# Attention stage: stores at the end of a step, a load queue in written order, norm weights at a group's turn

## The chip, the cores and the metric

The kernel runs on one core of a Trainium2 chip. A core has a matrix engine (TensorE, PE in the profile, with its weight loads as PEld), a vector engine (DVE), a scalar engine (ACT), a general engine (POOL) and a synchronisation engine (SP), which here does nothing but give out DMA transfers. Each engine takes its instructions strictly in the order in which they stand in its queue; semaphores tie the queues together. The metric is the device time of one execution in microseconds (us).

## The reference

One decoder layer on x of 2048 x 1024 in float32. The input is normalised and multiplied by one wide matrix. One branch is a chunked gated DeltaNet (after a short causal convolution); the other is a dilated sliding-window attention in three groups of four heads, which are merged by their softmax denominators. Both are gated, projected, merged by sigmoid gates, projected once more and added to x. What matters here is the attention branch:

```python
h = rms_norm(x, norm_w[layer])
proj = h @ w_in[layer]
...
sq = partial_rope(rms_norm(grp(swa_q), q_norm_w[layer][:, None, :]), cos, sin)
sk = partial_rope(rms_norm(grp(swa_k), k_norm_w[layer][:, None, :]), cos, sin)
sv = grp(swa_v)
for gi, (window, dilation) in enumerate(SWA_GROUPS):
    o_g, lse_g = dilated_window_attention(sq[:, :, gi], sk[:, :, gi], sv[:, :, gi], window, dilation)
```

The norm weights of queries and keys (q_norm_w, k_norm_w) differ by group, not by head. The dilations are 1, 4 and 16, so a block of 128 queries of groups 1 and 2 takes rows that lie 4 or 16 apart; the kernel therefore writes the projected rows to memory and reads them back in the order that the attention wants.

## The kernel before

Products of float32 are made of three products in a faster format: each operand is split into a high part (hh, wh) and a low part (hl, wl), and high x high, high x low and low x high are summed (L238 to L240). The high part is a copy on ACT, the low part a subtraction on DVE or POOL.

The attention stage is made of 12 units, a unit being one head of one group, with the groups in the order 2, 1, 0. A unit has 16 steps t, one per block of 128 rows, and a step has four parts j. Each part projects two of the eight k tiles (`s_proj`: 384 columns, queries, keys and values at once). In a step's part 1 the block of the step before gets its turn (`s_turn`: DVE multiplies by the inverse norm and the norm weights wqk, POOL applies the rotation in four instructions) and is stored (rscr<-rec). At the end of a step `s_norm` reads the projection: ACT takes the squares and the copy into rec, of which there are two buffers, and POOL makes the inverse norm. So the squares of step k + 2 wait until the store of step k has landed.

Attention blocks run between the parts of a step, some steps behind (`att_add` gives each its step, `at`): with d the step less `at`, the rows are loaded at d = -2 (qk<-rscr, v<-rscr), transposed at d = 0, scored at d = 1; at d = 2 the probabilities are transposed and multiplied with v, DVE copies the result into ol, and it is stored (oscr<-ol). What is left when the 12 units are done runs between the products of the next stage.

In the first unit the step also prepares x, one tile x(c) of 128 rows after the other (a list xq of events with their due quarter step). `x_next` takes ACT's squares of xt and POOL's power; `x_diag` puts the inverse norms on a diagonal (dg, ACT); `x_event` is a small PE product that spreads them over all partitions (tp, L120), followed by eight scalings on DVE (xc, L126); `x_parts` makes hh on ACT (L131) and hl in two pieces on DVE and POOL (L135), and then gives out the load of x(c + 3), whose buffer is free once hl of x(c) is made. `swa_first` does this for x(0) and splits the first unit's eight weight tiles (`high` on ACT, `low` on DVE for even and on POOL for odd tiles, L193).

The next unit's weights come in six raw tiles of 256 KB (`w384`, a generator that a step advances: in the first unit from step 12 on, in the others from step 6). There are three raw buffers.

PE, ACT, DVE and POOL follow the order in which the program is written (a manual schedule, switched on by `pinned`). In `swa_first` so does SP; in `swa_units` SP is left to the scheduler, which may give out a transfer earlier or later than it is written, as its dependencies allow.

## Time and profile before

| | |
|---|---|
| median of 3 runs | 2385.1 us (2384.5 to 2389.4) |
| the profiled execution | 2384.28 us, span 2382.4 us |
| PE busy, share of the span | 2343.1 us, 98% |
| ACT, DVE, POOL busy | 36%, 50%, 37% |
| share of the chain that ended last | PE 85%, POOL 4%, DMA 4%, DVE 4%, ACT 2% |
| mean granted TensorE clock | 0.996 |
| DMA | 307.30 MB, 129 GB/s over the span |

The attention stage covers about the first 1,020 us of the span. PE's busy time contains the overlap of matmuls that follow each other, so a busy PE is one that has no hole, not one at its peak. A row of a timeline has the start and the length in us, the engine, the line of the kernel, what is written from what, and in brackets how long the engine had been idle and what it waited for. SPq rows are transfers being given out; their landing is told by another view. Names are those of the program's tiles.

### The profile page before, as it was taken

The numbers are of one execution on the slowest core, as the hardware profiler recorded it, in microseconds if no ns is written. First come the engines' busy times: TensorE is split into PE (matmuls) and PEld (weight loads), VectorE is DVE, ScalarE is ACT, GpSimd is POOL, SyncE is SP. The second block draws the span as 40 slices with busy tenths as digits, with TensorE's granted clock in tenths as the row PEclk, the third lists the DMA queues.
The fourth block names the chain that finished last, engine by engine and source line by source line (L and its number), as shares of the span: only waits on it lengthen the run. The fifth ranks groups of instructions, "written<-read, shape, count | busy, mean of one in ns | idle before, by whom it ended". The sixth has DMA issues, their size and how long they took to land.

```text
span 2382.4 us, 40700 instructions
## 1 busy us (share of the span) xinstructions
PE 2343.1 (98%) x13640; PEld 2133.7 (90%) x13640; DVE 1191.4 (50%) x2831; ACT 847.5 (36%) x3021; POOL 886.0 (37%) x1855
## 2 busy tenths in 40 slices
PE   8999999999999999999999999999999999999999
PEld 7899999999999999988878888888888878889988
DVE  5543344334334434344877775999344433454431
ACT  6433333344444434333666662111233313111110
POOL 6633333333333334310855671101233212433441
PEclk9999999999999999999999999999999999999999
DMA  8443344333333335233544443222577645554542
GB/s 283 158 116 111 107 123 121 95 103 112 110 97 112 108 91 128 86 91 92 142 121 130 116 115 116 69 73 75 193 209 203 182 151 157 164 178 156 149 140 75
DMA packets 378808, 307.30 MB, mean 129 GB/s; under 512 B 61352, under 2 KB 345320, under 8 KB 378216
## 3 DMA queue, kind: packets, MB, share of 16 engines
q1 hardware_dynamic: 378312, 304.64, 43.6%
q8 instruction: 108, 1.77, 0.3%
q14 instruction: 100, 0.82, 0.1%
q10 hardware_dynamic: 288, 0.07, 0.0%
HBM read 187.92 MB, written 116.69 MB: 128 GB/s over the span
## 4 chain that ended last, share of the span: by engine, by line
PE 85%; POOL 4%; DMA 4%; DVE 4%; ACT 2%; issue 2%; SPq 0%; POOLq 0%; ACTq 0%; DVEq 0%
PE mm L240 10%; PE mm L238 10%; PE mm L239 10%; PE mm L524 9%; PE mm L526 9%; PE mm L525 9%; PE mm L1054 2%; PE mm L1052 2%; PE mm L1053 2%; PE mm L1035 2%; PE mm L1037 2%; PE mm L1036 2%; PE po L333 2%; PE tp L290 2%; DMA gcb<-gcscr 1%
## 5 line engine op out<-in xcount | busy, mean ns | idle before, releaser
L238 PE MATMUL mm<-wh,hh 128*128 128x384 f32 (+1 forms) x1536 | 555.0, 361 | 6.3 <-ACT hh L131 2.9
L240 PE MATMUL mm<-wh,hl 128*128 128x384 f32 (+1 forms) x1536 | 519.7, 338 | 1.7 <-DVE hl L135 1.7
L239 PE MATMUL mm<-wl,hh 128*128 128x384 f32 (+1 forms) x1536 | 518.3, 337 | 0.7 <-DVE wl L79 0.6
L524 PE MATMUL mm<-hh,wh 128*128 128x512 f32 x1152 | 464.1, 403 | 0.0
L526 PE MATMUL mm<-hh,wl 128*128 128x512 f32 x1152 | 454.7, 395 | 0.0
L525 PE MATMUL mm<-hl,wh 128*128 128x512 f32 x1152 | 451.4, 392 | 0.0
L238 PEld LDWEIGHTS mm<-wh,hh 128*128 128x128 f32 x1536 | 290.2, 189 | 10.8 <-ACT wh L78 4.4
L239 PEld LDWEIGHTS mm<-wl,hh 128*128 128x128 f32 x1536 | 291.0, 189 | 1.7 <-DVE wl L79 1.1
L240 PEld LDWEIGHTS mm<-wh,hl 128*128 128x128 f32 x1536 | 289.3, 188 | 2.6 <-DVE hl L135 2.6
L526 PEld LDWEIGHTS mm<-hh,wl 128*128 128x128 f32 x1152 | 217.0, 188 | 46.9
L525 PEld LDWEIGHTS mm<-hl,wh 128*128 128x128 f32 x1152 | 217.4, 189 | 41.8
L524 PEld LDWEIGHTS mm<-hh,wh 128*128 128x128 f32 x1152 | 217.2, 189 | 42.0
L263 DVE SCALAR_TENSOR_TENSOR rec<-mm,st,wqk 128x128 f32<-128x128 f32 x384 | 116.7, 346 | 263.7 <-POOL st L255 244.2
L79 POOL TENSOR_TENSOR wl<-raw,wh 128x512 fp32r<-128x512 f32 (+1 forms) x73 | 104.6, 1445 | 382.3 <-ACT wh L78 382.0
L317 ACT ACTIVATE p<-sc,ol 128x128 f32<-128x128 f32 (+1 forms) x192 | 82.1, 428 | 316.8 <-DVE ol L315 273.0
L253 POOL TENSOR_SCALAR st<-st 128x2 f32<-128x2 f32 x192 | 38.0, 198 | 399.7 <-ACT rec L249 398.2
L249 ACT ACTIVATE rec<-mm 128x128 f32<-128x128 f32 x384 | 102.7, 273 | 185.0 <-PE mm L240 171.8
L1035 PE MATMUL mm<-oh,hh 128*128 128x256 f32 x512 | 143.9, 281 | 2.9 <-DVE gt L1039 2.9
L1037 PE MATMUL mm<-oh,hl 128*128 128x256 f32 x512 | 142.9, 279 | 0.0
L1036 PE MATMUL mm<-ol,hh 128*128 128x256 f32 x512 | 142.9, 279 | 0.0
L255 POOL TENSOR_TENSOR st<-st,mhalf 128x2 f32<-128x2 f32 x192 | 135.0, 703 | 16.0
L632 DVE SCALAR_TENSOR_TENSOR acc<-xr,cw,acc 128x512 f32<-128x512 f32 x144 | 122.4, 850 | 17.4 <-ACT acc L630 12.4
(244 smaller groups left out, 4332.0 us busy)
## 6 DMA issues: line engine op xcount, KB each, us to landing
rscr<-rec SPq DMA_DIRECT2D x192, 192.0 KB, 1.9
raw<-in_w_in_dram SPq DMA_DIRECT2D x138, 256.0 KB, 3.1
qk<-rscr SPq DMA_DIRECT2D x192, 128.0 KB, 2.2
gscr<-gt SPq DMA_DIRECT2D x64, 256.0 KB, 2.4
gt<-gscr SPq DMA_DIRECT2D x64, 256.0 KB, 3.5
oscr<-ol SPq DMA_DIRECT2D x192, 65.0 KB, 2.0
oc<-oscr SPq DMA_DIRECT2D x16, 780.0 KB, 5.3
v<-rscr SPq DMA_DIRECT2D x192, 64.0 KB, 2.0
```

Of the source, the lines that this page charges most:

```text
L238: nc.tensor.matmul(pr[:, :w], a, wh[:, k, :w], start=(k == 0), stop=False)
L239: nc.tensor.matmul(pr[:, :w], a, wl[:, k, :w], start=False, stop=False)
L240: nc.tensor.matmul(pr[:, :w], b, wh[:, k, :w], start=False, stop=(k == KT - 1))
L255: nc.gpsimd.tensor_tensor(out=st[:, 2:4], in0=st[:, 0:2], in1=self.mhalf[:, 0:2], op=ALU.pow)
L263: nc.vector.scalar_tensor_tensor(out=qk[:, j, :], in0=pr[:, j * P:(j + 1) * P], scalar=st[:, 2 + j:3 + j], in1=s["w"][2][:, j, :], op0=ALU ...
L524: nc.tensor.matmul(pr, wh[:, k, :], a, start=(k == 0), stop=False)
L525: nc.tensor.matmul(pr, wh[:, k, :], b, start=False, stop=False)
L526: nc.tensor.matmul(pr, wl[:, k, :], a, start=False, stop=(k == KT - 1))
L632: nc.vector.scalar_tensor_tensor(out=acc, in0=xr[:, j:j + 512], scalar=w[:, j:j + 1], in1=acc, op0=ALU.mult, op1=ALU.add)
L1035: nc.tensor.matmul(o, self.wbh[:, k, ms], oh[:, k, :], start=(k == b * 4), stop=False)
L1036: nc.tensor.matmul(o, self.wbh[:, k, ms], ol[:, k, :], start=False, stop=False)
L1037: nc.tensor.matmul(o, self.wbl[:, k, ms], oh[:, k, :], start=False, stop=(k == b * 4 + 3))
```

## The change

- The store of the projected block (rscr<-rec) moves from the middle of a step, where its rotation is written, to the step's end, just ahead of that step's `s_norm`; the store of an attention block (oscr<-ol) moves from d = 2 to the first part of d = 3, and all attention runs one step later (`step + 4`).
- SP follows the written order in the whole attention stage (`pinned(True)`).
- The norm weights of a group are loaded in the first step of the group's first head, after the last block of the group before has had its turn, and no longer by the weight generator.
- At the start ACT copies the fourth weight tile and takes the squares of x(1) before the second half of x(0); the diagonal of x(1) comes ahead of weight tiles 4 to 7; and x(1)'s event is due at part 1 of the first step, not at part 0.

```diff
-        if h == 0:
-            self.wqk = self.sp.tile([P, 2, P], F32, name="wqk", bufs=1)
-            nc.sync.dma_start(self.wqk[:, 0, :], dr(i["q_norm_w"], g * P, [[0, P], [1, P]]))
-            nc.sync.dma_start(self.wqk[:, 1, :], dr(i["k_norm_w"], g * P, [[0, P], [1, P]]))
...
-                                           in1=s["w"][2][:, j, :], op0=ALU.mult, op1=ALU.mult)
+                                           in1=self.wqk[:, j, :], op0=ALU.mult, op1=ALU.mult)
...
-        nc.sync.dma_start(dr(self.rscr[s["h"]][g], t * P * 384, [[384, P], [1, 384]]), rec.rearrange("p a c -> p (a c)"))
+
+    def s_store(self, s):
+        self.nc.sync.dma_start(dr(self.rscr[s["h"]][s["g"]], s["t"] * P * 384, [[384, P], [1, 384]]),
+                               s["rec"].rearrange("p a c -> p (a c)"))
...
+
+    def a_store(self, a):
+        nc, g, u, ol = self.nc, a["g"], a["i"], a["ol"]
...
-            new = [(t, t > 0, step + 3)]
+            new = [(t, t > 0, step + 4)]
...
-            new = [(u, g == 1 and u % 4 > 0, step + 3) for u in range(16)]
+            new = [(u, g == 1 and u % 4 > 0, step + 4) for u in range(16)]
...
+            if which == 0 and d == 3:
+                self.a_store(a)
...
         self.x_low(0, 0, 4, nc.vector)
+        high(3)
+        self.x_stat(1)
         for k in (4, 6):
             self.x_scale(0, rows, k, k + 2)
             self.x_high(0, k, k + 2)
-        self.x_stat(1)
+        self.x_diag(1)
         self.x_low(0, 4, 8, nc.gpsimd)
         self.xc.pop(0)
         low(2)
         self.x_nat(2)
-        for k in range(3, 8):
+        low(3)
+        for k in range(4, 8):
             high(k)
             low(k)
-            if k == 4:
-                self.x_diag(1)
...
-        with pinned(False):
+        with pinned(True):
             self.swa_units(units, wps, xctx, w0)
...
-            xq += [(q, self.x_event, c), (q + 2, self.x_parts, c)]
+            xq += [(max(q, 1), self.x_event, c), (q + 2, self.x_parts, c)]
...
+                        if t == 0 and u % H == 0:
+                            self.wqk = self.sp.tile([P, 2, P], F32, name="wqk", bufs=1)
+                            for n, nm in enumerate(("q_norm_w", "k_norm_w")):
+                                nc.sync.dma_start(self.wqk[:, n, :], dr(self.i[nm], units[u][1] * P, [[0, P], [1, P]]))
...
+                if turn:
+                    self.s_store(turn)
                 self.s_norm(s)
...
         self.s_turn(turn)
+        self.s_store(turn)
```

The order on ACT at the start of the stage, before: hh of x(0) in four pieces, the squares of x(1) (xt_130), then the weight tiles (raw0_134 is the fourth, tile 3) with x(1)'s diagonal (dg) among them.

```order
L131 ACTIVATE hh_67<-xc_117 128x2x128 x4
L109 ACTIVATE xt_130,xst_199<-xt_130 128x1024
L190 ACTIVATE wh_121<-raw0_134 128x384
L190 ACTIVATE wh_121<-rec_136 128x384
L116 ACTIVATE dg_211<-ident_69,xst_199 128x128
L190 ACTIVATE wh_121<-rec_138 128x384
```

And now:

```order
L131 ACTIVATE hh_67<-xc_117 128x2x128 x2
L190 ACTIVATE wh_121<-raw0_134 128x384
L109 ACTIVATE xt_130,xst_194<-xt_130 128x1024
L131 ACTIVATE hh_67<-xc_117 128x2x128 x2
L116 ACTIVATE dg_204<-ident_69,xst_194 128x128
L190 ACTIVATE wh_121<-rec_136 128x384
```

Two of the four hh pieces now stand behind the fourth weight tile and the squares, and the diagonal stands ahead of the fifth weight tile. On POOL the order of the low parts is as it was: the low half of x(0) (hl), then the odd weight tiles from the fourth on. On PE the product tp of x(1) stood behind the products of k tiles 0 and 1 and now stands behind those of k tiles 0 to 3.

The order on SP in the first unit around steps 4 to 6, before. Here rec_564, rec_635 and rec_700 are the stores of steps 4, 5 and 6; xc_632, xc_697 and xc_756 the loads of x(10), x(11) and x(12); xt rows load the same tiles in the other layout.

```order
L275 DMA rscr02_86<-rec_564 128x384
L97 DMA xt_620<-in_x_dram 128x1024
L102 DMA xc_632<-in_xcol_dram 128x1024
L275 DMA rscr02_86<-rec_635 128x384
L97 DMA xt_679<-in_x_dram 128x1024
L102 DMA xc_697<-in_xcol_dram 128x1024
L97 DMA xt_744<-in_x_dram 128x1024
L275 DMA rscr02_86<-rec_700 128x384
L102 DMA xc_756<-in_xcol_dram 128x1024
```

And now, where the same loads are called xc_631, xc_696 and xc_755:

```order
L97 DMA xt_619<-in_x_dram 128x1024
L102 DMA xc_631<-in_xcol_dram 128x1024
L273 DMA rscr02_86<-rec_564 128x384
L97 DMA xt_678<-in_x_dram 128x1024
L102 DMA xc_696<-in_xcol_dram 128x1024
L273 DMA rscr02_86<-rec_635 128x384
L97 DMA xt_743<-in_x_dram 128x1024
L102 DMA xc_755<-in_xcol_dram 128x1024
L273 DMA rscr02_86<-rec_700 128x384
```

Each store has moved behind the xc load that it stood ahead of. The raw tiles of the second unit moved too: three of the six stood among these rows, ahead of the stores of steps 0 and 2, and now the first two stand behind the store of step 11.

## The prediction

> **What bounds the kernel now.** I read the table by stages first, then the timelines of the places where TensorE (PE) sits idle. In the table the columns are the stretch, its length, then each engine's busy time with its instructions, the granted clock, the DMA share and GB/s.
>
> ```profile
> 0.00:100.00 100.00, 84.56 (x454) 80.07 (x454) 61.15 (x186) 61.26 (x176) 70.32 (x146) 0.95 0.71 235
> 100.00:300.00 200.00, 198.55 (x1233) 196.84 (x1234) 74.38 (x286) 65.00 (x326) 81.03 (x247) 1.00 0.39 114
> ```
>
> The attention stage fills the first 1,020 us. From 100 us on PE has no hole worth naming (198.55 of 200 busy), and the other engines are under half busy, so moving their work, or a transfer that lands in time, changes nothing there. What can be won or lost lies in the first 100 us: 100 - 84.56 = 15.4 us of idle PE, while tiles of x are normalised for the first unit of projections. That is also the most a change of this stage can gain, about 0.65% of the run. Times below are us from the span's start; step k is the k-th row block of the first unit, x(c) the c-th tile of x.
>
> The first wait that the change touches, in the timeline of all engines (start, length, engine and line, in brackets the idle time before it and what ended it), and above it the transfer of the fourth weight tile:
>
> ```profile
> L186 SPq DMA_DIRECT2D raw<-in_w_in_dram x1: 442/442/442, 5.4 to 5.4; - x1
> DMA to landing us min/median/max: 6.2/6.2/6.2
> ```
>
> ```profile
> 11.16 0.93 ACT L131 ACTIVATE hh<-xc 128x256 fp32r<-128x256 f32 x2 [1.27 <-DVE xc L126]
> 12.00 1.04 ACT L109 ACTIVATE xt<-xt 128x1024 f32<-128x1024 f32 x1
> 13.04 0.51 ACT L190 ACTIVATE wh<-raw 128x384 fp32r<-128x384 f32 x1
> ...
> 14.02 1.66 POOL L135 TENSOR_TENSOR hl<-xc,hh 128x512 fp32r<-128x512 f32 x1
> 14.09 0.40 ACT L116 ACTIVATE dg<-ident,xst 128x128 f32<-128x128 f32 x1
> 14.54 0.80 PE L120 MATMUL tp<-dg,ones 128*128 128x128 f32 x2 [2.92 <-ACT dg L116]
> 15.38 0.61 DVE L126 SCALAR_TENSOR_TENSOR xc<-xc,nw,tp 128x128 f32<-128x128 f32 x2 [0.83 <-PE tp L120]
> 15.64 1.00 POOL L193 TENSOR_TENSOR wl<-raw,wh 128x384 fp32r<-128x384 f32 x1
> 16.70 0.69 PE L239 MATMUL mm<-wl,hh 128*128 128x384 f32 x1
> 16.98 1.63 DVE L126 SCALAR_TENSOR_TENSOR xc<-xc,nw,tp 128x128 f32<-128x128 f32 x6
> 19.35 1.66 POOL L135 TENSOR_TENSOR hl<-xc,hh 128x384 fp32r<-128x384 f32 x1 [0.46 <-ACT hh L131]
> 22.41 0.49 PE L120 MATMUL tp<-dg,ones 128*128 128x128 f32 x2 [1.13 <-ACT dg L116]
> 27.68 0.44 PE L238 MATMUL mm<-wh,hh 128*128 128x384 f32 x1 [1.41 <-ACT hh L131]
> ```
>
> PE waits 2.92 us for the row factors of x(1), and then, at 16.70, for something else: the low part of the fourth weight tile, which POOL makes last.
>
> **The start.** Three edits go together. ACT copies the fourth weight tile as third of its next jobs instead of after the squares of x(1), and x(1)'s factors (tp) stand on PE behind the third and fourth k tile instead of ahead of them. The fourth weight tile lands at 5.4 + 6.2 = 11.6, so ACT, in order, can no longer start the two hh copies at 11.16: it does the weight (0.51), the squares (1.04), the two hh (0.93) and is through at 11.6 + 0.5 + 1.0 + 0.9 = 14.0. POOL then takes the low half of x(0), 1.66, to 15.7, and the fourth weight's low part, 1.00, to 16.7. That is when it ended before (15.64 + 1.00), so PE gets no further by being given this work: its product of the fourth k tile still starts at about 16.7, and tp now stands behind it. Behind that product (0.69) and one more, tp runs at about 17.5, 3.0 later than 14.54. DVE's eight scalings of x(1) ran from 15.38 to 18.61 with a weight split among them; now they start 0.84 behind tp (15.38 - 14.54), at 18.3, and take 8 x 0.27 (1.63 for six) plus some 0.6 for the split, to 21.0, 2.4 later. The hh copy, POOL's low half of x(1) (19.35) and, behind it on POOL, x(2)'s factors (22.41) follow 2.3 later. SP's loads of x(4) wait for that low half too, so the start of step 2 at 27.68 follows as well. Nothing from there gives it back: every later step hangs on these, and the next PE wait of over 1 us, at 63.27 below, hangs on the same chain of DVE, ACT and POOL, which is late by as much. I take **+2.3**. Nothing in the chain becomes ready sooner, which excludes a gain here unless the clock moves (below); ends 0.8 and 4.0, that is 1.5 either way.
>
> **The stores.** Each rec store is now given out at a step's end, and SP keeps the program's order. In steady steps this costs nothing: the store waits for the same POOL result, and what stands behind it on SP (the attention loads, two steps ahead of use; the oscr store) has a step to spare. In the first unit it does cost, because the store now stands behind the 512 KB load of a later x tile, which waits for POOL. Here are three single transfers (the group with its start; then the time to landing), and the load that store 5 now follows:
>
> ```profile
> L102 SPq DMA_DIRECT2D xc<-in_xcol_dram x1: 327/327/327, 48.1 to 48.1; - x1
> DMA to landing us min/median/max: 5.2/5.2/5.2
> ```
>
> ```profile
> L275 SPq DMA_DIRECT2D rscr<-rec x1: 326/326/326, 49.2 to 49.2; - x1
> DMA to landing us min/median/max: 4.7/4.7/4.7
> ```
>
> ```profile
> L102 SPq DMA_DIRECT2D xc<-in_xcol_dram x1: 327/327/327, 63.8 to 63.8; - x1
> DMA to landing us min/median/max: 3.6/3.6/3.6
> ```
>
> ```profile
> 58.38 0.33 SPq L102 DMA_DIRECT2D xc<-in_xcol_dram  x1
> ```
>
> The store given out 1.1 us behind a load landed at 53.9, 0.6 behind the load (53.3), though a store alone lands in 1.9:
>
> ```profile
> rscr<-rec SPq DMA_DIRECT2D x192, 192.0 KB, 1.9
> raw<-in_w_in_dram SPq DMA_DIRECT2D x138, 256.0 KB, 3.1
> ```
>
> ACT's squares of step k + 2 write the buffer that store k empties, and ACT's order puts the row factors (dg) behind them:
>
> ```profile
> 60.12 0.26 ACT L249 ACTIVATE rec<-mm 128x128 f32<-128x128 f32 x1
> 62.82 0.40 ACT L116 ACTIVATE dg<-ident,xst 128x128 f32<-128x128 f32 x1 [1.92 <-POOL xst L112]
> 65.21 0.25 ACT L249 ACTIVATE rec<-mm 128x128 f32<-128x128 f32 x1
> 65.87 0.40 ACT L116 ACTIVATE dg<-ident,xst 128x128 f32<-128x128 f32 x1
> ```
>
> ```profile
> 63.27 0.49 PE L120 MATMUL tp<-dg,ones 128*128 128x128 f32 x2 [1.40 <-DVE xc L126]
> 67.81 0.38 PE L120 MATMUL tp<-dg,ones 128*128 128x128 f32 x2
> ```
>
> Store 5 now follows the load of 58.38: 58.38 + 3.6 + 0.6 = 62.6, where the squares of step 7 stood at 60.12. With 0.7 for the squares and their copy (65.21 to 65.87) dg is at 63.3 instead of 62.82, and PE, already waiting at 63.27, gets it 0.5 later. Store 6 follows the load of 63.8: 63.8 + 3.6 + 0.6 = 68.0 against 65.21, and dg at 68.7 against 65.87; PE's next tp stood at 67.81 and is held to 69.1 (dg and the 0.45 from 62.82 to 63.27), 1.3 in all. Two later stores are caught the same way (loads of x(14) and x(15)), with slack of some us ahead of PE; I add 0.7. Together **+2.0**, ends 0 (ACT's slack covers it) and 3.9 (the 2.5 and 2.8 by which these squares slip, less the 1.4 that PE waits at 63.27 anyway).
> Here the Trainium skill (DMA: Bandwidth & Descriptors, "Queues, rings and completion order") speaks against me: descriptors start in ring order, but completion is not first in, first out per issuing engine. By it a store need not wait for the load ahead; it would land at 58.8 + 1.9 = 60.7, dg would not move, and the sum would be 2.0 lower. The row above shows a store landing just behind its load, so I follow the row.
>
> **The second unit's weights.** The scheduler had loaded three of its six raw tiles far ahead; in fixed order the first two go at step 12, and the rest one by one behind a store.
>
> ```profile
> 96.76 0.44 PE L238 MATMUL mm<-wh,hh 128*128 128x384 f32 x1 [0.86 <-ACT wh L78]
> 101.17 0.45 PE L238 MATMUL mm<-wh,hh 128*128 128x384 f32 x1 [1.50 <-ACT wh L78]
> ```
>
> ```profile
> 93.81 0.99 SPq L206 DMA_DIRECT2D raw<-in_w_in_dram  x2
> ```
>
> PE already waits for the third (96.76) and sixth tile (101.17). The third would be given out at 93.81 and land 3.1 later, at 96.9, 0.8 behind its copy's place now (0.65 ahead of 96.76). The sixth waits for the third's split, so it slips by the same 0.8: **+0.8** at 101.17, not twice. Ends 0 and 1.0. From the next unit on two steps lie between a load and its split (9.9 us against 3.1), so zero.
>
> **The last unit.** One small wait there is hung on loads that the next stage sent ahead:
>
> ```profile
> 934.94 1.42 SPq L545 DMA_DIRECT2D cmask<-in_cmask_dram  x1
> ```
>
> ```profile
> 941.81 0.49 PE L332 MATMUL po<-v,pT 128*128 128x128 f32 x2 [1.31 <-ACT pT L326]
> ```
>
> The cmask load now stands between the store and these raw loads. Its 1.42 is a full queue behind four slow loads that would be over by then, so about 0.4 is left: **+0.4**, ends -1.3 and +1.4.
>
> **At nothing.** The norm weights now load in the first step of a group, after the last use of the old ones and almost a step ahead of the next; without that cover DVE would wait some 2 us, twice. Attention runs one step later: one step of unit 1 loses its share and one is added behind the last unit, where PE is just as full.
> **Sum.** 2.3 + 2.0 + 0.8 + 0.4 = 5.5. The profiled execution took 2384.3 (span 2382.4 and 1.9 around it), so **2389.8**. The lower ends add to -0.5 and the upper ones to 10.3: 2383.8 to 2394.6. That execution is 0.8 under the median of the runs shown, 2385.1. About 0.2%, 4.8 us, is what runs of this kernel can tell from no change; the forecast lies just at that edge.
>
> **Rivals.**
> *Covered.* ACT's slack takes up the stores, or they land past the load ahead of them, and the weights come in time for a stage that starts later: 2384.3 + 2.3 + 0.4 = 2387.0. For it: ACT is 61% busy in these 100 us. Against it: dg is wanted at once at 63.27.
> *Clock.* PE's clock was halved twice here:
>
> ```profile
> 11.70:18.50 6.80, 3.88 (x12) 3.38 (x13) 4.09 (x11) 4.52 (x10) 5.20 (x6) 0.50 1.09 373
> ...
> 28.70:32.10 3.40, 3.04 (x9) 3.04 (x10) 2.67 (x11) 2.64 (x6) 3.01 (x7) 0.51 0.71 209
> ```
>
> The second stretch did in 3.04 us what takes half, so it cost 1.5. Both follow idle PE. Now PE has still less to do up to 16.7 and waits again for x(1): one more such stretch gives 2389.8 + 1.5 = 2391.3.
> The Trainium skill (TensorE: Matmul & The Clock Gate, "What's actually happening") has the gate watch a free-running window of 3.4 us and halve the clock after an idle one; the trace's 3.40 agrees. An estimate from that page is 1.7 for one more window; where it falls can differ from run to run.
> *Faster.* If the fourth split were done before dg (14.5), PE would fill its 2.92 with the moved work and the half-clock stretch would shrink by the 1.9 it costs: 2384.3 - 2.9 - 1.9 = 2379.5. It decides on POOL: the split must come before POOL's 1.66 low half, and the order puts it behind.
> *Blocked queue.* In fixed order a late store could hold back weight loads in every unit; at the 1.31 of the last unit, ten times, 2384.3 + 13.1 = 2397.4. Against it: 9.9 us of lead for 3.1.
>
> **Chances.** Forecast 0.42, covered 0.24, clock 0.14, faster 0.12, blocked queue 0.08. Half of the forecast's own range (2387 to 2393), most of clock and all of the blocked queue are slower by over 0.2%: 0.21 + 0.12 + 0.07 = 0.40. Covered and the rest give 0.48 within 0.2%; faster 0.12. The range 2382 to 2396 takes in the ends of the sum and leaves out most of the last two rivals.
>
> **What would show it.** Right: the second tp on PE at about 17.5 with the wait before the fourth k tile's product, step 2 at about 30; in the list of waits, ACT's squares waiting for rscr more often; steady steps unchanged. Wrong: x(1)'s factors near 14.5; stores landing in 1.9 behind a load; new PE waits after 110 us; PE idle in the first 100 us below 15.4.

## The result and the profile after

| | before | after |
|---|---|---|
| median of 5 runs | 2385.1 us (2383.7 to 2389.4) | 2394.25 us (2392.9 to 2397.7) |
| ratio | 1 | 1.0036 (95% interval 1.0025 to 1.0047) |
| profiled execution: span | 2382.4 us | 2392.8 us |
| first unit of projections | 87.3 us | 95.0 us |
| end of the attention stage | 1019.7 us | 1026.6 us |

The changed kernel is slower by 9.2 us in the medians and by 10.4 us in the two profiled spans. The unit lengths are worked out from the starts of the products in the traces (24 matmuls a step, 16 steps a unit).

The stretches of the kernel after, in the columns of the prediction's first table:

```profile
0.00:100.00 100.00, 82.12 (x428) 76.78 (x429) 57.85 (x179) 57.20 (x163) 67.35 (x134) 0.93 0.67 220
100.00:300.00 200.00, 196.29 (x1212) 193.76 (x1210) 73.39 (x275) 65.86 (x326) 81.96 (x249) 1.00 0.40 114
```

PE has lost 2.4 us of its busy time in the first 100 us, and every other engine is less busy too: all of them wait more. In the next stretch the two waits at the start of the second unit, shown further down, come on top. The start of the kernel after, its rows for PE and those that it waits for:

```profile
16.60 0.69 PE L235 MATMUL mm<-wl,hh 128*128 128x384 f32 x1 [3.03 <-POOL wl L193]
...
17.41 0.63 PE L120 MATMUL tp<-dg,ones 128*128 128x128 f32 x2
...
21.44 1.65 POOL L135 TENSOR_TENSOR hl<-xc,hh 128x384 fp32r<-128x384 f32 x1 [2.97 <-ACT hh L131]
...
24.48 0.49 PE L120 MATMUL tp<-dg,ones 128*128 128x128 f32 x2 [1.03 <-ACT dg L116]
...
29.64 0.44 PE L234 MATMUL mm<-wh,hh 128*128 128x384 f32 x1 [1.29 <-ACT hh L131]
```

The wait stands ahead of the fourth k tile's product, the row factors of x(1) run at 17.41 and not at 14.54, and step 2 starts at 29.64 instead of 27.68. How much of this is left at step 3 depends on where a stretch of half clock falls. Five of the profiles of this document have one inside step 2 (before and, of the runs told below, u_start, undo3, rec3 and late_dn), and there step 2 takes 6.9 to 7.0 us. The kernel after has none there (granted clock 1.00 between 27 and 38 us, against 0.84 before), its step 2 takes 5.5 us, and its step 3 starts only 0.6 us later than before (35.13 against 34.55). The stretch around step 2, before and after, in the columns of the first table:

```profile
27.00:38.00 11.00, 9.55 (x47) 9.24 (x47) 7.26 (x23) 8.18 (x26) 9.17 (x21) 0.84 0.85 255
```

```profile
27.00:38.00 11.00, 8.95 (x51) 8.44 (x50) 7.07 (x23) 6.82 (x17) 8.10 (x18) 1.00 0.62 212
```

The second place is steps 4 to 9. They took 28.9 us before and take 34.6 now. ACT's row of waits for a store in the list of waits for 30 to 104 us, before and after (in total, times, longest):

```profile
ACT rec L249 <- DMA rscr<-rec: 4.6, 1, 4.6
```

```profile
ACT rec L245 <- DMA rscr<-rec: 16.2, 6, 4.0
```

What that wait does, in the timeline after. First a store, the two loads ahead of it on SP, and its time to landing from the view of its line:

```profile
37.14 0.33 SPq L102 DMA_DIRECT2D xc<-in_xcol_dram  x1
37.56 0.38 SPq L97 DMA_DIRECT2D xt<-in_x_dram  x1
37.99 0.42 SPq L273 DMA_DIRECT2D rscr<-rec  x1
```

```profile
L273 SPq DMA_DIRECT2D rscr<-rec x1: 423/423/423, 38.0 to 38.0; - x1
...
DMA to landing us min/median/max: 6.1/6.1/6.1
```

Then the chain behind the landing of the store before it, which ends in a wait of PE:

```profile
38.15 0.28 ACT L245 ACTIVATE rec<-mm 128x128 f32<-128x128 f32 x1 [2.03 <-DMA rscr<-rec]
...
39.14 0.70 POOL L251 TENSOR_TENSOR st<-st,mhalf 128x2 f32<-128x2 f32 x1
...
39.88 0.61 DVE L259 SCALAR_TENSOR_TENSOR rec<-mm,st,wqk 128x128 f32<-128x128 f32 x2 [2.31 <-POOL st L251]
...
40.41 0.81 DVE L135 TENSOR_TENSOR hl<-xc,hh 128x640 fp32r<-128x640 f32 x1
...
41.27 0.44 PE L236 MATMUL mm<-wh,hl 128*128 128x384 f32 x1 [1.12 <-DVE hl L135]
```

ACT's squares wait for the store; POOL's inverse norm waits for the squares; DVE's turn waits 2.31 us for that; and the low part of the next x tile stands behind the turn on DVE. PE waits for this low part. Further on PE waits for a low part again (at 62.00; DVE's turn had waited 1.99 us for the inverse norm at 57.75, and the scalings of the next x tile, their copy on ACT and the low part stood behind it), and for the row factors:

```profile
62.00 0.45 PE L236 MATMUL mm<-wh,hl 128*128 128x384 f32 x1 [1.16 <-DVE hl L135]
...
68.43 0.49 PE L120 MATMUL tp<-dg,ones 128*128 128x128 f32 x2 [2.08 <-ACT dg L116]
...
86.74 0.49 PE L120 MATMUL tp<-dg,ones 128*128 128x128 f32 x2 [1.28 <-ACT dg L116]
```

The start of the second unit, and the one wait of the last unit:

```profile
104.36 0.44 PE L234 MATMUL mm<-wh,hh 128*128 128x384 f32 x1 [1.73 <-ACT wh L78]
...
108.70 0.44 PE L234 MATMUL mm<-wh,hh 128*128 128x384 f32 x1 [1.42 <-ACT wh L78]
```

```profile
948.72 0.49 PE L331 MATMUL po<-v,pT 128*128 128x128 f32 x2 [1.91 <-ACT pT L325]
```

The third place was in no part of the prediction. The next stage (DeltaNet) runs units of four row blocks of 512 columns; I count its row blocks from 0. At row block 12 the program drains what is left of attention, closes attention's memory and opens DeltaNet's in the same place; the first thing loaded there is gcb. Before and after, SP's, DVE's and PE's rows around it:

```profile
1111.23 8.25 SPq L338 DMA_DIRECT2D oscr<-ol  x4
1119.53 8.35 SPq L651 DMA_DIRECT2D gcb<-gcscr  x2
...
1126.30 1.14 DVE L662 SCALAR_TENSOR_TENSOR E<-gcb,ngc 128x128 f32<-128x128 f32 x4 [2.35 <-POOL gcb L655]
...
1137.11 0.44 PE L688 MATMUL tp<-ident,kT 128*128 128x128 f32 x2 [1.37 <-DVE kT L637]
```

```profile
1117.69 11.10 SPq L340 DMA_DIRECT2D oscr<-ol  x5
1128.83 0.43 SPq L663 DMA_DIRECT2D gcb<-gcscr  x1
...
1136.76 1.14 DVE L674 SCALAR_TENSOR_TENSOR E<-gcb,ngc 128x128 f32<-128x128 f32 x4 [5.32 <-POOL gcb L667]
...
1139.81 0.41 PE L700 MATMUL tp<-ident,kT 128*128 128x128 f32 x2 [2.10 <-DVE kT L649]
...
1147.67 0.44 PE L700 MATMUL tp<-ident,kT 128*128 128x128 f32 x2 [1.69 <-DVE kT L649]
```

Five attention blocks instead of four are stored there. The gcb load is given out 9.3 us later, though the stage as a whole is only 6.5 us later, DVE waits 5.32 us for gcb instead of 2.35, and PE waits twice for kT behind it.

In numbers: the first unit lost 7.7 us; the second unit gave back 0.9 (one attention block fewer); the ten units after it moved the end of the stage by +0.1 in all (the sixth is 0.5 shorter, the last 0.6 longer); the first twelve row blocks of the next stage gave back 0.4; row blocks 12 to 16 lost 4.1, of which 0.6 came back by row block 28. That is 10.0 in all. At the last row block of that stage the difference is 8.9 and at the end of the span 10.4; what moves it there is not shown.

### The profile page after: what moved, and what is told of

It reads as the page before. It is cut to its first block, busy times and chain, and to the rows that moved or that the text cites. A ratio compares the mean times of both kernels' runs of the same rounds, so it can differ in the third digit from the quotient of the medians.

```text
span 2392.8 us, 40603 instructions
## 1 busy us (share of the span) xinstructions
PE 2346.7 (98%) x13640; PEld 2134.9 (89%) x13640; DVE 1193.0 (50%) x2831; ACT 846.6 (35%) x3021; POOL 886.8 (37%) x1855
## 4 chain that ended last, share of the span: by engine, by line
PE 83%; DMA 4%; POOL 3%; DVE 3%; issue 3%; ACT 2%; SPq 0%; POOLq 0%; ACTq 0%; DVEq 0%
PE mm L236 10%; PE mm L234 10%; PE mm L235 10%; PE mm L536 9%; PE mm L538 8%; PE mm L537 8%; PE mm L1066 2%; PE mm L1064 2%; PE mm L1065 2%; PE mm L1047 2%; PE mm L1049 2%; PE mm L1048 2%; PE po L332 2%; PE tp L289 2%; PE tp L323 1%
```

## The experiments

All ratios are to the kernel before; the change itself stands at 1.0036. The columns are worked out from the starts of the products in each trace, so each stands for one execution. The intervals reach about 0.001 to either side, 2.4 us, so the ratios of two of these kernels that lie 0.0012 apart or less do not tell them apart; what the single edits do is read from the traces, and the ratios only go along with them.

| run | start of step 2 | steps 4 to 9 | first unit | last unit | row blocks 12 to 16 against before | median, us | ratio (95%) |
|---|---|---|---|---|---|---|---|
| before | 27.7 | 28.9 | 87.3 | 88.6 | 0 | 2385.1 | 1 |
| after | 29.6 | 34.6 | 95.0 | 89.2 | +4.1 | 2394.3 | 1.0036 (1.0025 to 1.0047) |
| u_store | 30.0 | 30.2 | 90.2 | 92.1 | +4.5 | 2394.5 | 1.0040 (1.0027 to 1.0052) |
| u_start | 27.8 | 32.3 | 91.9 | 88.5 | +4.1 | 2392.6 | 1.0029 (1.0018 to 1.0041) |
| u_shift | 29.7 | 33.8 | 94.3 | 88.3 | -0.1 | 2392.4 | 1.0024 (1.0014 to 1.0034) |
| rec3 | 29.9 | 28.7 | 90.2 | 88.9 | +4.5 | 2390.0 | 1.0017 (1.0008 to 1.0026) |
| undo3 | 27.8 | 28.7 | 88.4 | 88.2 | -0.1 | 2386.5 | 1.0001 (0.9992 to 1.0010) |

The start and the stores can be told apart at the start of step 10, which lies behind all steps of the second place. Against before it comes 5.5 to 6.3 us later with both (after, u_shift, and the runs wearly and late_dn below), 3.7 with the stores alone (u_start), 2.2 with the start alone (rec3, u_store), and 0.1 with neither (undo3). So the start costs 1.9 to 2.6 us there and the wait for the stores 3.3 to 4.1, and the two add up.

**The store back in the middle of a step (u_store).**

```diff
                         self.s_turn(turn)
+                        self.s_store(turn)
...
-                if turn:
-                    self.s_store(turn)
                 self.s_norm(s)
```

> One part undone: the rec store goes back to the middle of a step, right behind the turn that makes it; start order, attention shift, norm weights and SP in written order stay as changed. Theory 'stores' (the store now stands behind a 512 KB load of an x tile, lands behind it, and ACT's squares of step k + 2 wait for it): steps 4 to 9 of the first unit, 34.6 us in the changed kernel and 28.9 before, go back to 29 to 30.5, the list of ACT's waits for rscr between 30 and 78 us falls from 7.1 us to under 2, and the time is 4 to 6 us under the changed kernel's 2394.3, some 2389 (+0.15% on before). Theory 'late start' (the x tiles are 2 us late from step 2 on, and the waits of steps 4 to 9 are that lateness coming out): steps 4 to 9 stay at 33 or more and the time stays above 2393.

In the first unit this is what "stores" said: steps 4 to 9 take 30.2 us, no wait of ACT for rscr is left between 30 and 78 us, and the unit is 4.8 us shorter. The time, 2394.5, is not, and that part of the expectation missed. The profile is of the slowest of the five runs (2399.4 us). In it PE loses time in the last unit, where a weight tile of the next stage lands late, and ACT, in order, stands before it:

```profile
944.48 0.63 ACT L78 ACTIVATE wh<-raw 128x512 fp32r<-128x512 f32 x1 [5.09 <-DMA raw<-in_w_in_dram]
...
945.44 0.49 PE L331 MATMUL po<-v,pT 128*128 128x128 f32 x2 [3.19 <-ACT pT L325]
```

PE's 3.19 us here were 1.91 after and 1.31 before. Half-clock stretches followed at 946 and at 1223 us, which the kernel after does not have there; what they cost is not taken apart from the late tile. Whether the other four runs have either is not on record, so why the median did not fall stays open.

**The start order back (u_start).**

```diff
-        high(3)
-        self.x_stat(1)
         for k in (4, 6):
...
-        self.x_diag(1)
+        self.x_stat(1)
         self.x_low(0, 4, 8, nc.gpsimd)
...
+            if k == 4:
+                self.x_diag(1)
...
-            xq += [(max(q, 1), self.x_event, c), (q + 2, self.x_parts, c)]
+            xq += [(q, self.x_event, c), (q + 2, self.x_parts, c)]
```

> One part undone: the three edits at the start (order of the fourth weight tile, squares and diagonal of x(1), and its event's due time); stores at a step's end, attention shift and SP in written order stay. Theory 'late start': step 2 starts at 27.7 as before and not at 29.6, steps 4 to 9 fall back to near 29 with it, and the time falls by 5 us or more, to 2389 or less. Theory 'stores': step 2 starts at 27.7, steps 4 to 9 keep 33 to 35, and the time falls by 0 to 2.3 us only, to 2392 to 2394 (the half-clock stretches, 3.4 us each, can shift this by 1.6 either way).

Step 2 starts at 27.8 and the ratio falls by 0.0007, that is 1.7 us, a fall that is not clear of noise by itself; steps 4 to 9 keep most of their delay, so "stores" holds and "late start" falls. They stand at 32.3, below the 33 to 35 expected. The same steps of four kernels that share the change's start and stores (after, u_shift, wearly and late_dn) took 34.6, 33.8, 33.8 and 32.6 us, so of these 2.3 us about 1 to 2 is scatter of one profiled execution; part of it comes from the clock, for late_dn, with its half-clock stretch in step 2, starts step 4 1.7 us later than after.

**Attention three steps behind again (u_shift).**

```diff
-            if "qk" not in a and (d == 0 or (d == -2 and which == 1)):
+            if "qk" not in a and (d == 0 or (d == -1 and which == 0)):
...
-            new = [(t, t > 0, step + 4)]
+            new = [(t, t > 0, step + 3)]
...
-            new = [(u, g == 1 and u % 4 > 0, step + 4) for u in range(16)]
+            new = [(u, g == 1 and u % 4 > 0, step + 3) for u in range(16)]
```

> One part undone: attention blocks stand three steps behind again instead of four; since the stores stay at a step's end, the rows are then loaded at the step before their transposes instead of two ahead. Theory 'handover' (the last attention block ends one step later in the next stage, its oscr store holds SP's in-order queue until 1128.8, and the gcb load behind it lands at 1135.4 where DVE waits 5.3 us for it): row blocks 13 to 16 of the next stage, which lost 4.1 us against before, lose under 1, gcb is given out some 9 us sooner, and the time falls by 3 to 4 us, to about 2390.5. The first unit keeps its 95.0 us. Rival, that this loss belongs to SP's order in general: blocks 13 to 16 still lose 3 or more and the time stays within 1 us of 2394.3.

The rows of DVE and PE behind the hand-over, after this edit:

```profile
1132.88 1.14 DVE L674 SCALAR_TENSOR_TENSOR E<-gcb,ngc 128x128 f32<-128x128 f32 x4 [2.19 <-POOL gcb L667]
```

```profile
1143.76 0.44 PE L700 MATMUL tp<-ident,kT 128*128 128x128 f32 x2 [1.27 <-DVE kT L649]
```

DVE's wait for gcb is 2.19 us again and one of PE's two waits is gone; row blocks 12 to 16 lose nothing (-0.1 instead of +4.1). gcb is given out at 1126.29, 2.5 us sooner than after; the "9 us sooner" of the expectation counted the stage's own lateness, and missed. The ratio falls by 0.0012, 2.9 us, which by itself is not clear of noise. That the loss sits at the hand-over and comes from the shift is shown by the traces: row blocks 12 to 16 lose 3.7 to 5.2 us in all seven kernels that have the shift and the hand-over where the change has it, and nothing in u_shift and undo3, which do not have the shift. Of the 4.1 us, 1.4 fall on row block 12 (one more attention block runs in it; the second unit is 0.9 shorter for that) and 2.7 on the waits for kT.

**Three rec buffers (rec3).**

```diff
...
-        rec = sp.tile([P, 3, P], F32, name="rec", bufs=2)
+        rec = sp.tile([P, 3, P], F32, name="rec", bufs=3)
...
-        pT = a["pT"] = sp.tile([P, 256], F32, name="pT", bufs=2)
+        pT = a["pT"] = sp.tile([P, 256], F32, name="pT", bufs=1)
```

> The changed kernel with three rec buffers instead of two (the fourth raw weight tile of the start uses the third one, and pT has one buffer instead of two, to pay for it): ACT's squares of step k + 2 no longer wait for store k but for store k - 1. The stores themselves stay where the change put them. Theory 'stores' in its narrow form (only the wait of the squares for the store costs anything): steps 4 to 9 fall from 34.6 to 29 to 30, no wait of ACT for rscr is left between 30 and 78 us, and the time falls by 4 to 6 us to about 2389. If what costs is the stores' crowding of the load queue instead (the x tiles land later because SP stands waiting for a store's rotation), steps 4 to 9 stay above 32 and the time above 2392.

ACT's waits between 30 and 78 us, all of them:

```profile
ACT hh L131 <- DVE xc L126: 7.2, 11, 2.5
ACT dg L116 <- POOL xst L112: 4.3, 4, 1.9
ACT rec L243 <- ACT xt L109: 1.0, 1, 1.0
ACT rec L243 <- PE mm L234: 0.9, 2, 0.6
```

None is for rscr, steps 4 to 9 take 28.7 us, and the ratio falls by 0.0019, 4.5 us, the largest fall of the three parts; its interval (to 1.0026) only just touches that of the change (from 1.0025). The stores stand where the change put them, so their late landing by itself is harmless: only the wait of the squares for it costs. This run also shows the two other terms of the first unit without the stores: step 3 starts 2.3 us later than before (36.9 against 34.55; both have a half-clock stretch in step 2), and step 15 takes 6.06 us instead of 5.30.

**All three taken back (undo3)**, the edits of u_start, u_shift and rec3 together.

> The changed kernel with three things taken back at once: the start order, the attention shift (with the rows loaded one step ahead of their transposes), and the wait of the squares for the store (three rec buffers). Left of the change: the stores' late place, SP in written order, the norm weights' place. If the parts found so far are all there is and they add up, only the second unit's raw weights (+0.8) and the last unit's raw loads (+0.3 to 0.6) are left: the first unit takes 88 to 88.5 us (87.3 before), the row blocks of the next stage lose nothing more, and the time is 0.5 to 1.5 us over before, ratio 1.000 to 1.001. If something else of SP's written order costs, the ratio stays at 1.0015 or above.

The ratio is 1.0001 (0.9992 to 1.0010) and the first unit 88.4 us, with its last step at 6.33 instead of 5.30 us. The three single falls add to 0.0038 and the joint one is 0.0035: the parts add up, and the stores' late place, the norm weights' place and SP's written order cost at most about 0.1% together when nothing waits for them.

**Is it the queue or the engines? (store_actq, probe2q).** The prediction had the store late because it stands behind a load in SP's queue. The first try gave the store out from ACT:

```diff
-        self.nc.sync.dma_start(dr(self.rscr[s["h"]][s["g"]], s["t"] * P * 384, [[384, P], [1, 384]]),
+        self.nc.scalar.dma_start(dr(self.rscr[s["h"]][s["g"]], s["t"] * P * 384, [[384, P], [1, 384]]),
```

> The changed kernel with one thing altered: the rec store, at the same place at a step's end, is given out by ACT on its own queue instead of by SP. ACT does not wait for the rotation there, which POOL has done half a step before. Theory 'ring' (a store lands late because it stands in SP's queue behind the 512 KB load of an x tile): given out on another queue at the same time it lands in 1.9 to 2.5 us although the load is in flight, ACT's waits for rscr between 30 and 78 us (7.1 us) go, steps 4 to 9 of the first unit (34.6) fall to 29 to 30.5, and the time falls by 4 to 5 us to about 2390. Theory 'shared engines' (the 16 DMA engines are busy with the load's rows whatever the queue): the store still lands 4 to 6 us after it is given out, steps 4 to 9 stay at 33 or more, and the time stays near 2394.

The stores land in 1.9 us (median of the seven with a recorded landing, of nine between 33 and 82 us), yet steps 4 to 9 take 32.1 us and the time is 2397.8 (ratio 1.0051, 1.0037 to 1.0064). The expectation was wrong on a fact: in the first unit POOL does not have the rotation done half a step before, and ACT now stands still until it has:

```profile
65.16 0.25 POOL L270 TENSOR_TENSOR rec<-t,t 128x32 f32<-128x32 f32 x1
65.44 0.33 ACTq L273 DMA_DIRECT2D rscr<-rec  x1
65.87 0.28 ACT L245 ACTIVATE rec<-mm 128x128 f32<-128x128 f32 x1 [2.12 <-DVE xc L126]
```

The idle 2.12 us end just behind the store, which came 0.03 us behind the end of the rotation, whatever the row names. So most of these stores are also given out later against the loads than SP's were, when a load is nearly through, and their 1.9 us don't tell the queue from the engines. One of them is not: given out at 53.41, 1.35 us behind an x load of SP's, it took 5.7 us on ACT's queue. The second try leaves the kernel after as it is and adds stores of the same form on ACT's queue:

```diff
...
+                if u == 0 and 3 <= t < 13:
+                    nc.scalar.dma_start(dr(self.probe, t * P * 384, [[384, P], [1, 384]]),
+                                        self.rope[:, 0:12, :].rearrange("p a c -> p (a c)"))
                 self.s_norm(s)
```

> The changed kernel with a second store of the same form added to ten steps of the first unit (128 rows of 1.5 KB from a constant tile to a scratch of its own), given out by ACT on its queue at the same place in a step, a step's end, where SP gives out the rec store behind the loads of the x tiles. It waits for nothing and nothing waits for it. Theory 'ring' (a store lands half a us behind the load ahead of it in its own queue, whatever the engines could do): SP's stores land in 4 to 6 us and about 0.5 behind the load ahead, the added ones in 1.9 to 2.5 us. Theory 'shared engines' (the store waits for its share of the DMA engines, which both queues have in common): both land in 4 to 6 us while two loads are in flight, and in 2 when none is.

The transfers given out between 33 and 82 us in this run (KB each, median us to landing):

```profile
xc<-in_xcol_dram SPq DMA_DIRECT2D x10, 512.0 KB, 4.2
xt<-in_x_dram SPq DMA_DIRECT2D x9, 512.0 KB, 5.2
rscr<-rec SPq DMA_DIRECT2D x9, 192.0 KB, 4.8
probe<-rope ACTq DMA_DIRECT2D x8, 192.0 KB, 4.9
```

4.9 us on a queue with no load in it, against 4.8 behind the loads: "ring" falls, and both kinds land as "shared engines" said for loads in flight. Of the eight added stores the landings of four are recorded (4.3 to 5.3 us, where "ring" said 1.9 to 2.5), and two of the four come 0.5 us behind a transfer of SP's queue, as SP's own stores come behind their loads (0.50 to 0.53 us in the five pairs of the kernel after with both landings recorded). That it is the DMA engines that the queues share, and not the memory behind them, no run separates. One run gave 2396.5 us, on which nothing rests.

**The second unit's raw tiles a step sooner (wearly).**

```diff
-                if u + 1 < nu and t >= (12 if u == 0 else 6):
+                if u + 1 < nu and t >= (11 if u == 0 else 6):
...
-                    for _ in range((1, 3, 2, 2)[t - 12] if u == 0 else 1):
+                    for _ in range((1, 2, 2, 2, 1)[t - 11] if u == 0 else 1):
```

> The changed kernel with the raw weight tiles of the second unit given out from step 11 on instead of 12, spread one, two, two, two, one over the steps instead of one, three, two, two. If the waits at the start of the second unit (1.73 us for the third tile's copy and 1.42 for the sixth in the changed kernel, 0.86 and 1.50 before) come from late raw loads alone, both go, and the second unit starts about 1.7 us sooner and its first step is 1.4 shorter: 2394.3 - 3.1 = 2391. If the splits are late because ACT and DVE are still busy with the last x tiles, the two waits keep more than half of their 3.2 us and the time moves by less than 1.5.

A miss. The wait at the second unit's start went, and a longer one came in its first step:

```profile
106.72 0.44 PE L234 MATMUL mm<-wh,hh 128*128 128x384 f32 x1 [2.36 <-ACT wh L78]
```

The third unit starts at 183.0 us instead of 183.5, and the time did not move: 2394.6 (ratio 1.0036, 1.0023 to 1.0048). Each raw tile but the first three needs the buffer of one that has been split, so loads and splits follow each other whenever they begin. Whether ACT's place for the last split or the landing decides I did not separate.

**The hand-over one unit later (late_dn).**

```diff
-        first, rest = zu[:3], zu[3:] + gu
-        self.cunits(first + du + rest, {3: open_dn, 15: lambda: self.at(9, start_inverse)}, tail)
+        first, rest = zu[:4], zu[4:] + gu
+        self.cunits(first + du + rest, {4: open_dn, 16: lambda: self.at(9, start_inverse)}, tail)
```

> The changed kernel with four projection units instead of three ahead of the point where the next stage takes over the memory of attention; the rest of attention thus finds four more row blocks to run between. Nothing else moves. Theory 'handover' (one more attention block runs at that point with no projection between, and the gcb load, which takes attention's memory, lands late behind it): from the stage's start to row block 28 the kernel loses no more than before plus 0.5, where the changed kernel loses 3.1 more (from +6.9 to +10.0); and since the blocks that before drained there without cover are covered too, the time falls by 3 to 6 us, to 2388.5 to 2391. Rival, that the 3 us belong to the first DeltaNet blocks themselves whatever stands ahead: they move to a later row block and the time stays within 1.5 us of 2394.3.

2389.1 us, ratio 1.0014 (1.0005 to 1.0024): 5.2 us less than after, inside the expected 3 to 6. From the stage's start to the last of its 144 row blocks it is 3.1 us shorter than before, where the kernel after is 2.0 longer (and u_shift, without the loss at the hand-over, 2.0 as well, so this length scatters by a few us); row block 28, which the expectation named, no longer holds the same work, so I compare at the end. It gains more than the shift cost. The expectation's reason, that blocks that drained without cover before the change are covered too, fits, but no run takes it apart.

**A version that beats both (best)**: the kernel before with the edits of wearly and late_dn, and at the start (`low` gets the engine as an argument)

```diff
         self.x_low(0, 0, 4, nc.vector)
+        self.x_stat(1)
         for k in (4, 6):
             self.x_scale(0, rows, k, k + 2)
             self.x_high(0, k, k + 2)
-        self.x_stat(1)
+        self.x_diag(1)
...
-        for k in range(3, 8):
-            high(k)
-            low(k)
-            if k == 4:
-                self.x_diag(1)
+        high(3)
+        low(3, nc.vector)
...
+        def w_rest(_):
+            for k in range(4, 8):
+                high(k)
+                low(k)
...
+        xq.insert(1, (0, self.w_rest, 0))
```

> Not the changed kernel but the kernel before with three other edits, after what the runs point at: (1) at the start ACT takes the squares of x(1) between the two halves of x(0), x(1)'s diagonal follows, DVE instead of POOL makes the low part of the fourth weight tile, and weight tiles 4 to 7 are split behind the scalings of x(1); (2) the second unit's raw tiles from step 11 on; (3) four projection units ahead of the hand-over instead of three. If PE's 2.92 us wait at 14.54 goes and step 2 starts at 25 instead of 27.7: -2.5 to -4 with the clock; the two weight waits -2.4; the drain and the gcb wait -3 to -5: 8 to 11 us in all, 2375 to 2378 against 2385.5. If the start is bound by landing transfers (x(1) lands at 10.9 and the raw tiles from 11.6 to 14.3), edit (1) gives under 1 and the sum is 5 to 7, some 2379.

2379.9 us, ratio 0.9974 (0.9963 to 0.9984): faster than the kernel before by about 6 us, the second case of the expectation. Most of what the traces place lies behind the attention stage, whose end comes 2.1 us sooner: from the next stage's start to its last row block it gains 3.3 us more. The first unit is only 1.2 us shorter, 1.0 of it in its last step. The start did not come out as meant: x(1)'s factors ran at 14.33, since ACT stood 1.35 us before a raw tile that had not landed.

```profile
12.44 0.52 ACT L190 ACTIVATE wh<-rec 128x384 fp32r<-128x384 f32 x1 [1.35 <-DMA rec<-in_w_in_dram]
...
14.33 0.80 PE L120 MATMUL tp<-dg,ones 128*128 128x128 f32 x2 [2.22 <-ACT dg L116]
```

The copies of weight tiles 4 and 5, written in `swa_units`, came ahead of the second half of x(0), written in `swa_first`: these are two separately ordered pieces of the program, and in this trace the order of the one did not hold the other back.

## Why the prediction was right or wrong, point by point

The sign, the place of most of the loss (the first 100 us) and the range were right; the forecast was 4.5 us short of the median, one of its four terms was mis-sized, another is not borne out, and a fifth was missing. That the range took in the time, near its upper end, is owed to its width and not to the missing term having been thought of.

- **The start, +2.3: right.** tp at 17.41 (forecast 17.5), the wait ahead of the fourth k tile's product, step 2 at 29.64 (about 30). In all eight kernels with this start, probe2q and store_actq among them, step 2 starts 2.0 to 2.3 us later than before, and in the two without it 0.1, so the mechanism and the size hold. Without the stores' delay it is 2.3 us at step 3 (rec3) and 2.2 at step 10. "Nothing from there gives it back" did not hold in the profile after: with the clock full in step 2, 0.6 is left at step 3, which is luck of that execution. In the time, undoing the start gave 1.7 us, not clear of noise.
- **The stores, +2.0, ends 0 and 3.9: mis-sized, at or past its upper end.** Undoing the wait gives the first unit 4.8 us back (95.0 to 90.2), or 3.5 with the start undone as well (91.9 to 88.4), and the ratio 0.0019, 4.5 us. The mechanism is the one forecast, ACT's squares waiting for a store behind a load. Two steps of the working failed. It followed the late squares to one consumer only, the row factors (dg); the other, POOL's inverse norm, then DVE's turn, then the low part of the next x tile, gave the wait at 41.27 and, by a longer way, that at 62.00: in the list of PE's waits for 30 to 104 us, the low parts on DVE stand at 3.8 us (0.3 before) and the row factors on ACT at 4.2 (0.2 before, when 1.4 more was put down to DVE's scalings). And it began with store 5, when the store given out at 37.99 already took 6.1 us, behind two loads and not one.
- **Against the rule: the row was right, my reason was not.** The prediction followed the row that shows a store landing 0.6 us behind its load, and explained it by the queue. The probe shows the same delay on another queue. The Trainium skill (DMA: Bandwidth & Descriptors, "Queues, rings and completion order") says also that SP and ACT each own one ring on each of the same 16 engines, and that a transfer's completion mark lands only after every earlier write of that engine, across its queues; 4.9 against 4.8 us agrees. From the same section I had taken only the sentence that completion is not first in, first out, and worked out 60.7 for store 5 from it, as if a store beside a load were a store alone.
- **The second unit's weights, +0.8: right in size, wrong in place.** The whole of it came at the third tile (0.86 to 1.73), and the sixth did not slip (1.50 to 1.42).
- **The last unit, +0.4: not borne out.** This profile has the wait longer (1.31 to 1.91), with the raw loads behind the cmask load as forecast, but the same wait is 1.24 in u_start, 1.05 in u_shift and 1.00 in undo3, which keep SP's written order, and 1.60 in rec3: the 0.6 lies within what it scatters.
- **Attention one step later, at nothing: wrong.** The step that failed is "one is added behind the last unit, where PE is just as full". What is added falls at the point where attention's memory is handed over, with the gcb load behind it: +4.1 us in the trace against the 0.9 that the second unit gives back, 2.9 us in the ratio when undone.
- **Covered** (0.24) fell: ACT is 57% busy in these 100 us and still had no slack, for it stood waiting. **Blocked queue** (0.08) did not come: the units between the second and the last are within 0.5 us of before. In u_store one weight load lands late, in the last unit (3.19 us of PE's wait); whether a store held it back is not shown. **Faster** fell: POOL's low half stood ahead of the split, as its own condition said.
- **Clock** (0.14): the kernel after has 3.4 us more of half clock in the first 35 us (13.65 us against 10.24). So has undo3, with the start as before and a time equal to before's. The share of full clock in its first 100 us is the same as after:

```profile
0.00:100.00 100.00, 85.64 (x451) 81.09 (x452) 60.99 (x185) 60.88 (x176) 69.39 (x143) 0.93 0.71 232
```

So the longer half-clock time is not what the change cost. What matters is the place: a stretch in step 2 costs about 1.5 us (7.0 against 5.5), before has paid it there and after has not, so in this pair of profiles the clock, by its place, goes the other way at step 3.

## What to carry to other kernels

Follow a late result to everything that waits for it on every engine, in order, and not only to the consumer nearest to the bottleneck: here PE waited nearly as long at the end of the second path (3.8 us) as of the first (4.2). When work is moved later by one step, look at where the last piece of it ends, since a hand-over of memory there makes everything behind it wait. A transfer that is late because of traffic was here made harmless by one more buffer, not by another place or queue: with the stores in their old place or on ACT's queue the time did not fall.

## What the runs showed of the hardware that I had not expected

A 192 KB store given out among 512 KB loads took 4.9 us on a queue of its own (median of four) and 4.8 us behind the loads (median of nine), against a median of 1.9 over a whole run before and after: the queue did not matter. Apart from the one cut off by the end of the span, the half-clock stretches in all profiles here are 3.41 us or small multiples of it (6.83, 10.24, 13.65), and lie elsewhere in each profile: in the first 35 us they began at 11.7 and 28.7 before, at 9.1 after, at 9.0 and 29.5 in undo3.
